# A two-layer hybrid trunk: opening the first FFN chunk by chunk, and other tiles in front of the mixers' late steps

## The chip, the cores and the metric

The kernel runs on one core of a Trainium2 chip. The metric is the device time of one execution in microseconds (us), lower is better. The time of the kernel before is the median of three runs.

## The reference, cut to what matters

The trunk has two layers for one sequence of S = 256 tokens with D = 1024 channels. Layer 0 is an FFN, a pooling and SSD mixer ("AB"), an FFN; layer 1 is an FFN, a multi-head latent attention ("MLA"), an FFN. Every sub-layer has its own shift, scale and gate, three rows of a matrix product with the vector `c`:

```python
c_act = jax.nn.silu(c)
for i in range(DEPTH):
    mod = c_act @ mod_w[i] + mod_b[i]
    sh1, sc1, g1, sh2, sc2, g2, sh3, sc3, g3 = jnp.split(mod, 3 * N_SUB, axis=-1)
    h = modulate(rmsnorm(x, norm_g[i, 0]), sh1, sc1)      # h * (1 + scale) + shift
    x = x + FFN_RES * g1[:, None, :] * swiglu(h, ffn_w13[i, 0], ffn_w2[i, 0])
    h = modulate(rmsnorm(x, norm_g[i, 1]), sh2, sc2)
    m = pool_ssd_mixer(h, ...) if i % 2 == 0 else mla_mixer(h, ...)
    x = x + g2[:, None, :] * m
    h = modulate(rmsnorm(x, norm_g[i, 2]), sh3, sc3)
    x = x + FFN_RES * g3[:, None, :] * swiglu(h, ffn_w13[i, 1], ffn_w2[i, 1])
return rmsnorm(x, final_norm_g)
```

`swiglu` is silu(h @ w1) * (h @ w3) @ w2 with 2816 inner channels. The SSD mixer ends in a norm over two groups of 512 channels and one output projection over 512 pooled and 1024 SSD channels. The attention has 16 heads, a causal mask and a softmax.

## The kernel before, in words

**Layout.** Activations lie transposed: 8 chunks of 128 channels on the partitions, 256 tokens along the free axis. Weights stream from HBM in tiles `raw` of 1 MiB (16 blocks of 128 x 128), six buffers, issued by SP in the order of a list `items`. Each half of a weight tile is split for exactness: ScalarE casts it to `wh` (L222), VectorE subtracts to get the rest, `wl` (L223), with five buffers of each; VectorE's subtraction waits for ScalarE's cast. The activation is split alike into `hh` and `hl`. One 128 x 128 product of a tile takes three matmuls (wl x hh, wh x hl, wh x hh, L522), or two where `hh` and `hl` lie side by side in `hx`: one of 512 columns (L266) and one of 256 (L267).

**Modulation.** A row of `mod_w` for one chunk of 128 channels is one VectorE instruction over 128 x 1024 with `c` (L210), which sums into one column of `modc`. These rows are items of the list too, set between the weights. `process_half` takes the next half item of the list, whatever it is; `take` hands out blocks and works ahead by four halves (one in the opening). A tile framework orders the instructions by their program order, pools and dependences; on TensorE, VectorE and ScalarE they run in that order.

**The opening** (`first_pairs`). The first FFN's first 16 output tiles of 256 columns (`n`, eight PSUM banks) are opened while `c`'s rows still come in. Chunks 0 and 1 of `h` are scaled (`scaled`, L500: scale L503, multiply L506, shift L293, then ScalarE's `h` L508 and cast L509) and meet f32 weight blocks directly (L532); then the other half of the tiles follows for these chunks (`part(1, 0)`); then three times a pair of chunks: four modulation rows, two `scaled`, two low parts (L512), four halves of weights, and `part` for all 16 tiles. Then the FFN goes on with full tiles `a` and `b` of 512 columns (L266, L267), and the down projection `f`, whose tiles end in VectorE's `residual` (L446).

**The AB mixer** runs a loop of eight turns: a transpose of `xs` (`tok_tile`), two heads' decay matrices, a `z` tile (in the turns 2 to 5), the products `y` (L818). After the first turn come the pooling tiles: `u`, its copy `utok`, then `pd` (L769) and `pw`. At turn 6 the first group norm is summed and its root taken by a Newton step on VectorE (`newton_r`). At the end some output tiles `o` are opened over their four pooled chunks (OPEN_A = 4 of 8, in three cuts CUT_A), while the second group's sum (`ss_g`, L321) and the split of its channels (`hx`, L315) are made; then all cuts are closed, each tile by two residual steps (L446) and the first steps of the next norm (`ul`, L376).

**The MLA mixer** makes q, k and v tiles, then eight turns of two heads: `scores` (`s`, L1077, softmax with Exp on ScalarE L1086, L1087), `attend_t` (transposes `pt`, copied to `pT` by ScalarE, L1099), a q tile for a later turn (`q_tiles`, with the copy `qr` L1058 and its rotation `rotq` L1005 on even turns), k tiles in the turns 0 and 1, `attend_o` (`o`, L1105, L1108). The output projection opens three tiles over six chunks after the loop, then finishes the last turn, then closes.

Of the kernel before, what the change touches and what calls it, by code (L numbers as in the profile page):

```python
# [61 lines left out]
def trunk(ctx, tc, xT, c_row, pos, kc, cols, rows, mod_w, w13s, w13, w2, win_a, wdt,  # L62
# [124 lines left out]
    def last_vector():  # L187
# [3 lines left out]
        return None  # L191

    def process_half():
# [10 lines left out]
        if it[0] == "m":  # L204
            _, l, v, b, halves = it
            hf = halves[hf]
            c0 = l * 72 + v * 8 + b * 2 + hf
# [6 lines left out]
            last = hf == halves[-1]  # L214
            done_mod[(l, v, 2 * b + hf)] = True
        else:
            lo, hi = hf * PT, min((hf + 1) * PT, it[2])
            n = (hi - lo) * P
            wh = wp.tile([P, PT * P], F32R, tag="wh", name=f"wh{i}_{hf}")
            wl = wp.tile([P, PT * P], F32R, tag="wl", name=f"wl{i}_{hf}")  # L220
            src = r[:, lo * P : hi * P]
            A.copy(wh[:, :n], src)  # L222
            V.tensor_tensor(out=wl[:, :n], in0=src, in1=wh[:, :n].bitcast(F32), op=ALU.subtract)  # L223
            pieces.append((wh, wl, hi - lo))
# [1115 lines left out]
```

## Time and profile before

| | us |
|---|---|
| three runs | 1026.05, 1029.26, 1035.23 |
| median | 1029.26 |
| the profiled execution's own time | 1032.29 |
| its span in the trace | 1030.5 |
| TensorE busy | 1010.1 (98%) |
| VectorE busy | 887.4 (86%) |
| ScalarE busy | 617.6 (60%) |

The span runs from the first to the last recorded instruction; 1.8 us lie around it. Times in the rows below count from the span's start. PE is TensorE, DVE VectorE, ACT ScalarE. The mean granted clock of TensorE is 0.993 of its full 2.4 GHz.

### The profile page before, as it was taken

The numbers are of one execution on the slowest core, as the hardware profiler recorded it, in microseconds if no ns is written. First come the engines' busy times: TensorE is split into PE (matmuls) and PEld (weight loads), VectorE is DVE, ScalarE is ACT, GpSimd is POOL, SyncE is SP. The second block draws the span as 40 slices with busy tenths as digits, with TensorE's granted clock in tenths as the row PEclk, the third lists the DMA queues.
The fourth block names the chain that finished last, engine by engine and source line by source line (L and its number), as shares of the span: only waits on it lengthen the run. The fifth ranks groups of instructions, "written<-read, shape, count | busy, mean of one in ns | idle before, by whom it ended". The sixth has DMA issues, their size and how long they took to land.

```text
span 1030.5 us, 16634 instructions
## 1 busy us (share of the span) xinstructions
PE 1010.1 (98%) x6300; PEld 895.1 (87%) x6300; DVE 887.4 (86%) x1665; ACT 617.6 (60%) x1124; POOL 0.2 (0%) x4
## 2 busy tenths in 40 slices
PE   9899999999999999999999999999999999999997
PEld 7898888889887988888898888889988798888886
DVE  6888999998998898989979988999988689877653
ACT  3475564448896666565447665555678666655542
POOL 0000000000000000000000000000000000000000
PEclk9999999999999999999999999999999999999999
DMA  9987989976743468788875887798643246766501
GB/s 353 397 311 283 354 296 377 342 294 223 261 164 123 164 227 304 273 296 332 300 262 176 316 292 264 298 342 304 247 175 118 77 164 220 270 214 236 184 21 41
DMA packets 38642, 254.93 MB, mean 247 GB/s; under 512 B 4241, under 2 KB 6817, under 8 KB 8738
## 3 DMA queue, kind: packets, MB, share of 16 engines
q1 hardware_dynamic: 38562, 253.88, 67.9%
q8 instruction: 49, 0.80, 0.3%
q14 instruction: 31, 0.25, 0.1%
HBM read 252.79 MB, written 1.06 MB: 246 GB/s over the span
## 4 chain that ended last, share of the span: by engine, by line
PE 85%; DVE 9%; ACT 3%; DMA 1%; issue 1%; SPq 0%; DVEq 0%; ACTq 0%
PE f L266 14%; PE a L266 13%; PE b L266 13%; PE f L267 7%; PE a L267 6%; PE b L267 6%; PE o L266 4%; DVE wl L223 3%; DVE raw L210 3%; PE o L267 2%; PE n L522 1%; PE s L1077 1%; DMA raw<-in_w13s 1%; PE u_a L260 1%; PE u_b L261 1%; PE u_a L261 1%
## 5 line engine op out<-in xcount | busy, mean ns | idle before, releaser
L222 ACT CAST wh<-raw 128x1024 fp32r<-128x1024 f32 x327 | 339.1, 1049 | 247.0 <-PE f L266 71.6
L223 DVE TENSOR_TENSOR wl<-raw,wh 128x1024 fp32r<-128x1024 f32 x327 | 396.2, 1218 | 77.8 <-ACT wh L222 77.3
L266 PE MATMUL f<-g,wh 128*128 128x512 f32 x704 | 245.7, 395 | 0.0
L266 PE MATMUL a<-hx,wh 128*128 128x512 f32 x568 | 202.9, 396 | 0.0
L266 PE MATMUL b<-hx,wh 128*128 128x512 f32 x568 | 202.7, 396 | 0.0
L267 PE MATMUL f<-g,wl 128*128 128x256 f32 x704 | 195.7, 279 | 1.1 <-DVE wl L223 1.1
L210 DVE SCALAR_TENSOR_TENSOR raw<-raw,c_bc 128x1024 f32<-128x1024 f32 x144 | 170.7, 1217 | 0.5 <-DMA raw<-in_mod_w 0.5
L266 PEld LDWEIGHTS f<-g,wh 128*128 128x128 f32 x704 | 131.9, 188 | 31.0
L267 PE MATMUL a<-hx,wl 128*128 128x256 f32 x568 | 158.4, 279 | 0.0
L267 PE MATMUL b<-hx,wl 128*128 128x256 f32 x568 | 158.4, 279 | 0.0
L267 PEld LDWEIGHTS f<-g,wl 128*128 128x128 f32 x704 | 132.4, 188 | 2.0 <-DVE wl L223 1.8
L266 PEld LDWEIGHTS b<-hx,wh 128*128 128x128 f32 x568 | 106.6, 188 | 25.3
L266 PEld LDWEIGHTS a<-hx,wh 128*128 128x128 f32 x568 | 106.6, 188 | 25.3 <-DVE hx L401 0.3
L267 PEld LDWEIGHTS a<-hx,wl 128*128 128x128 f32 x568 | 107.0, 188 | 0.3
L267 PEld LDWEIGHTS b<-hx,wl 128*128 128x128 f32 x568 | 107.0, 188 | 0.3
L266 PE MATMUL o<-hx,wh 128*128 128x512 f32 x128 | 47.2, 410 | 0.7 <-DVE hx L315 0.7
L375 ACT ACTIVATE uh<-xt,gs_t 128x256 fp32r<-128x256 f32 x40 | 20.3, 507 | 43.5 <-DVE xt L446 43.4
L314 ACT CAST g<-g 128x256 fp32r<-128x256 f32 x88 | 35.2, 404 | 17.2 <-DVE g L593 10.4
L522 PE MATMUL n<-hx,wh 128*128 128x256 f32 x224 | 41.9, 289 | 0.0
L446 DVE SCALAR_TENSOR_TENSOR xt<-f,gt_t,xt 128x256 f32<-128x256 f32 x64 | 30.7, 480 | 12.7 <-PE f L267 12.4
L315 DVE TENSOR_TENSOR g<-g,g 128x256 fp32r<-128x256 f32 x88 | 36.6, 418 | 1.9 <-ACT g L314 1.9
L522 PE MATMUL n<-hx,wl 128*128 128x256 f32 x112 | 32.9, 294 | 4.8 <-DVE wl L223 4.8
(397 smaller groups left out, 1683.5 us busy)
## 6 DMA issues: line engine op xcount, KB each, us to landing
raw<-in_w SPq DMA_DIRECT2D x124, 1024.0 KB, 5.0
raw<-in_mod_w SPq DMA_DIRECT2D x70, 1024.0 KB, 5.1
raw<-in_win_a SPq DMA_DIRECT2D x12, 1024.0 KB, 7.0
raw<-in_w13s SPq DMA_DIRECT2D x7, 1024.0 KB, 10.2
raw<-in_wout_a SPq DMA_DIRECT2D x6, 1024.0 KB, 4.7
raw<-in_wq SPq DMA_DIRECT2D x5, 1024.0 KB, 5.2
raw<-in_win_m SPq DMA_DIRECT2D x4, 1024.0 KB, 5.2
raw<-in_wo SPq DMA_DIRECT2D x4, 1024.0 KB, 4.8
```

The lines of the kernel that those rows point to most:

```text
L210: V.scalar_tensor_tensor(out=sl, in0=sl, scalar=1.0, in1=c_bc, op0=ALU.mult, op1=ALU.mult, accum_out=modc[:, c0 : c0 + 1])
L222: A.copy(wh[:, :n], src)
L223: V.tensor_tensor(out=wl[:, :n], in0=src, in1=wh[:, :n].bitcast(F32), op=ALU.subtract)
L260: T.matmul(pt, wl, xh, start=first, stop=False)
L261: T.matmul(pt, wh, xl, start=False, stop=False)
L266: T.matmul(pt, wh, x, start=first, stop=False)
L267: T.matmul(pt[:, S:], wl, x[:, 0], start=False, stop=last)
L314: A.copy(dh, src)
L315: V.tensor_tensor(out=dl, in0=src, in1=dh.bitcast(F32), op=ALU.subtract)
L375: A.activation(uh[:, c, :S], x, AF.Identity, bias=0.0, scale=g)
L446: V.scalar_tensor_tensor(out=xt[:, d], in0=pt[:, e * S : (e + 1) * S], scalar=gate[:, d : d + 1], in1=xt[:, d], op0=ALU.mult, op1=ALU.add)
L522: T.matmul(tile_of(m), w, x[:, k], start=k == 0 and m % 2 == 0 and w is wl, stop=k == NC - 1 and w is wh and x is hh, skip_group_check=True)
```

## The change

Opening: the items of the list are now, for each chunk, the scale row and the shift row together (two transfers of 0.5 MiB into one buffer) and one weight tile with all 16 output tiles' blocks of that chunk. A small table `colh` with what the opening needs is loaded first; the large one, `colt`, moves behind the opening's loads. The scale and the shift of a chunk are made by ScalarE. In each round `cast_half(1)` casts the weight halves ahead of their turn, and VectorE runs: two rows, the multiply, the first `wl`, the low part of `h`, the second `wl`. The low part of chunk 0 comes before the rows of chunk 1.

AB mixer: the first group norm moves from turn 6 to turn 5, behind the `z` tile; the pooling tiles from turn 1 to turn 2; six output tiles are opened for four. MLA mixer: the third k slab is made before the first scores, the fourth in turn 1; an Exp of one column stands before the scores; the output projection has three cuts (4, 6, 8), and its first tiles are opened in the turns 6 and 7, its last open tile before the last transposes. Two casts for the mask move in VectorE's order to their place in the program. The host lays out the weights for the new orders.

```diff
-CUT_A, OPEN_A = (4, 8, 12), 4
+CUT_A, OPEN_A = (4, 8, 12), 6
...
-G0_AT = 6
+G0_AT = 5
...
-CUT_M, OPEN_M = (6, 8), 3
+CUT_M, OPEN_M = (4, 6, 8), 3
...
     items = []
     for c in range(2):
-        items += [mod_block(0, 1, 0, (c,)), mod_block(0, 0, 0, (c,)),
-                  ("f", w13s[0, 0][:, 8 * P * c : 8 * P * c + 8 * P], 8)]
-    items.append(("w", w13s[1, 0], 16))
-    for b in range(1, 4):
-        items += [mod_block(0, 1, b), mod_block(0, 0, b)]
-        items += [("w", w13s[q, b], 16) for q in range(NSETS)]
+        items += [("m", ((0, 1, c), (0, 0, c))), ("f", w13s[0][:, 8 * P * c : 8 * P * c + 8 * P], 8)]
+    items.append(("w", w13s[1], 16))
+    for c in range(2, NC):
+        items += [("m", ((0, 1, c), (0, 0, c))), ("w", w13c[c - 2], 16)]
...
-    nc.sync.dma_start(colt, cols)
+    nc.sync.dma_start(colh, colsh)
     def late_loads():
+        nc.sync.dma_start(colt, cols)
...
+                (l, v, c), other = it[1]
+                if other == (l, v, c + 1):
+                    nc.sync.dma_start(r, mod_w[l, v, c // 2])
+                else:
+                    for e, (l, v, c) in enumerate(it[1]):
+                        nc.sync.dma_start(r[:, e * D : e * D + D], mod_w[l, v, c // 2][:, c % 2 * D : c % 2 * D + D])
...
+    def cast_half(ahead):
+        i = state["item"] + ahead
+        hf = state["cast"] if ahead else state["half"]
+        issue_dma(min([i] + held) + RAHEAD - 1)
+        it, r = items[i], raws[i]
+        lo, hi = hf * PT, min((hf + 1) * PT, it[2])
+        n = (hi - lo) * P
+        wh = wp.tile([P, PT * P], F32R, tag="wh", name=f"wh{i}_{hf}")
+        wl = wp.tile([P, PT * P], F32R, tag="wl", name=f"wl{i}_{hf}")
+        src = r[:, lo * P : hi * P]
+        A.copy(wh[:, :n], src)
+        state["cast"] = 1 - hf
+        return wh, wl, src, n
+
+    def low_half(c):
+        wh, wl, src, n = c
+        V.tensor_tensor(out=wl[:, :n], in0=src, in1=wh[:, :n].bitcast(F32), op=ALU.subtract)
+        pieces.append((wh, wl, n // P))
...
+        def scale(c):
+            A.activation(gs_t[:, 0, c : c + 1], modc[:, 8 + c : 9 + c], AF.Identity, bias=b1[:, c : c + 1],
+                         scale=colh[:, 16 + c : 17 + c])
...
+        scale(0)
...
         def scaled(c):
-            m, b = mod_col(0, 1, (c, c + 1))
-            g = gs_t[:, 0, c : c + 1]
-            V.scalar_tensor_tensor(out=g, in0=m, scalar=b1[:, c : c + 1], in1=colt[:, CP_NG + c : CP_NG + c + 1],
-                                   op0=ALU.add, op1=ALU.mult)
+            assert done_mod.get((0, 0, c)) and done_mod.get((0, 1, c))
+            g, sh = gs_t[:, 0, c : c + 1], sh_t[:, 0, c : c + 1]
             t = tmp(f"h{norm.key}_{c}")
             V.tensor_tensor(out=t, in0=xt[:, c], in1=r, op=ALU.mult)
-            sh = prep_shift(0, 0, (c, c + 1))[:, c : c + 1]
+            A.activation(sh, modc[:, c : c + 1], AF.Identity, bias=colh[:, c : c + 1])
             A.activation(h[c], t, AF.Identity, bias=sh, scale=g)
             A.copy(hh[:, c], h[c])
...
-        def part(q, b):
-            for m in range(8 * q, 8 * q + 8):
-                for k in (2 * b, 2 * b + 1):
-                    wh, wl = take()
-                    for w, x in ((wl, hh), (wh, hl), (wh, hh)):
-                        T.matmul(tile_of(m), w, x[:, k], start=k == 0 and m % 2 == 0 and w is wl,
-                                 stop=k == NC - 1 and w is wh and x is hh, skip_group_check=True)
+        def mm(m, k, w):
+            for w_, x in ((w[1], hh), (w[0], hl), (w[0], hh)):
+                T.matmul(tile_of(m), w_, x[:, k], start=k == 0 and m % 2 == 0 and w_ is w[1],
+                         stop=k == NC - 1 and w_ is w[0] and x is hh, skip_group_check=True)
 
         for c in range(2):
             if c:
                 process_half()
+                scale(1)
                 process_half()
             scaled(c)
             w = next_raw()
@@ -532,23 +554,25 @@
                 T.matmul(tile_of(m), w[:, m * P : (m + 1) * P], h[c], start=c == 0 and m % 2 == 0, stop=False,
                          skip_group_check=True)
             release_raw()
-        low(0)
+            if c == 0:
+                low(0)
         low(1)
-        process_half()
-        process_half()
-        part(1, 0)
-        for b in range(1, 4):
+        for m in range(8, 16):
+            for k in range(2):
+                mm(m, k, take())
+        for c in range(2, NC):
+            first = cast_half(1)
             process_half()
+            scale(c)
+            second = cast_half(1)
             process_half()
-            process_half()
-            scaled(2 * b)
-            process_half()
-            low(2 * b)
-            scaled(2 * b + 1)
-            process_half()
-            low(2 * b + 1)
-            for q in range(NSETS):
-                part(q, b)
+            scaled(c)
+            low_half(first)
+            low(c)
+            low_half(second)
+            skip_item()
+            for m in range(2 * NS):
+                mm(m, c, take())
...
-            if i == G0_AT:
-                r0 = newton_r("g0", gss[0], 1.0 / 512)
             if i < 8:
                 tok_tile(i)
                 nxt_h = (i, heads(i))
@@ -866,11 +888,13 @@
                 u_part(3)
             elif i < 6:
                 z_tile(i + 2)
+            if i == G0_AT:
+                r0 = newton_r("g0", gss[0], 1.0 / 512)
             ymm(*prev)
             if i < 5:
                 gate_y(i - 1)
             prev = nxt_h
-            if i == 1:
+            if i == 2:
...
+        d = sp.tile([P, 1], F32, tag="wsq", name="wexp", bufs=1)
+        A.activation(d, nqs[:, 0:1], AF.Exp)
...
+        k_tiles(2)
+        proj = OutProj(CUT_M, OPEN_M, lambda k: hx[:, k])
         prev = None
         for i in range(8):
             prs = scores(i)
@@ -1118,20 +1150,23 @@
                 attend_t(*prev)
             if i + NQ - 1 < 8:
                 q_tiles(i + NQ - 1)
-            if i < 2:
-                k_tiles(2 + i)
+            if i == 1:
+                k_tiles(3)
+            if i >= 6:
+                proj.part(i - 6, 0, CUT_M[0])
             if prev is not None:
                 attend_o(prev[0])
             prev = (i, prs)
         gate = prep_gate(l, 1)
         nxt = make_next()
 
-        proj = OutProj(CUT_M, OPEN_M, lambda k: hx[:, k])
         proj.target(gate, nxt)
-        proj.cut(0)
+        for d in range(2, OPEN_M):
+            proj.part(d, 0, CUT_M[0])
         attend_t(*prev)
+        proj.cut(1)
         attend_o(prev[0])
-        proj.cut(1)
+        proj.cut(2)
```

The order of the instructions on VectorE in the opening, from the third chunk on. Before (`raw` L210 rows of the modulation, `gs_t` scale, `h` the multiply, `sh_t` shift, `hx` low part, `wl` low weights):

```order
L210 SCALAR_TENSOR_TENSOR raw_197,modc<-raw_197,c_bc 128x1024 x2
L210 SCALAR_TENSOR_TENSOR raw_207,modc<-raw_207,c_bc 128x1024
L503 SCALAR_TENSOR_TENSOR gs_t<-modc,b_136,colt 128x1
L506 TENSOR_TENSOR h_0_2_297<-xt,r_first 128x256
L293 TENSOR_TENSOR sh_t<-modc,colt 128x1
L210 SCALAR_TENSOR_TENSOR raw_207,modc<-raw_207,c_bc 128x1024
L512 TENSOR_TENSOR hx<-h_190,hx 128x256
L503 SCALAR_TENSOR_TENSOR gs_t<-modc,b_136,colt 128x1
L506 TENSOR_TENSOR h_0_3_305<-xt,r_first 128x256
L293 TENSOR_TENSOR sh_t<-modc,colt 128x1
L223 TENSOR_TENSOR wl_0_313<-raw_210,wh_0_312 128x1024
```

And now, two rounds of one chunk each (L236 modulation, L530 multiply, L213 low weights, L536 low part):

```order
L236 SCALAR_TENSOR_TENSOR raw_172,modc<-raw_172,c_bc 128x1024 x2
L530 TENSOR_TENSOR h_0_2_302<-xt,r_first 128x256
L213 TENSOR_TENSOR wl_0_294<-raw_199,wh_0_293 128x1024
L536 TENSOR_TENSOR hx<-h_193,hx 128x256
L213 TENSOR_TENSOR wl_1_299<-raw_199,wh_1_298 128x1024
L236 SCALAR_TENSOR_TENSOR raw_210,modc<-raw_210,c_bc 128x1024 x2
L530 TENSOR_TENSOR h_0_3_372<-xt,r_first 128x256
L213 TENSOR_TENSOR wl_0_364<-raw_221,wh_0_363 128x1024
L536 TENSOR_TENSOR hx<-h_193,hx 128x256
```

The scale and shift rows are gone from VectorE, the first low weights stand behind two modulation rows instead of four, and the next rows only behind the second low weights.

The order on TensorE where the pooling tiles begin. Before, behind the last `u` product and one turn's `y`:

```order
L757 MATMUL u_2805<-wh_1_2898,hx 128x512
L818 MATMUL y_3014<-lm_2194,xtk_2189 64x256 x2
L821 MATMUL y_3014<-lm_2194,xtk_2190 64x128 x2
L769 MATMUL pd_3022<-raw_2644,utok 128x128
L770 MATMUL pd_3022<-raw_2644,utok 128x128
L771 MATMUL pd_3022<-raw_2644,utok 128x16
```

And now, one turn later, behind a `z` tile:

```order
L282 MATMUL z_3043<-hx,wh_0_2940 128x256
L842 MATMUL y_3073<-lm_2201,xtk_2195 64x256 x2
L845 MATMUL y_3073<-lm_2201,xtk_2196 64x128 x2
L793 MATMUL pd_3083<-raw_2650,utok 128x128
L794 MATMUL pd_3083<-raw_2650,utok 128x128
L795 MATMUL pd_3083<-raw_2650,utok 128x16
```

Between the last `u` product and the first `pd` there are now a further transpose, a `z` tile and a further `y`.

The order on ScalarE at the first scores of the attention (`pe` is the Exp, `qr` the copy that `rotq` reads, `qh` copies of q). Before:

```order
L1086 ACT_TABLE_LOAD
L1086 ACTIVATE pe_7844,st_8225<-s_8215,st_8225,rqs 128x128
L1087 ACTIVATE pe_7844,st_8225<-s_8215,st_8225,rqs 128x256
L1086 ACTIVATE pe_7844,st_8234<-s_8216,st_8234,rqs 128x128
L1087 ACTIVATE pe_7844,st_8234<-s_8216,st_8234,rqs 128x256
L1058 COPY qr<-qr_8243 128x256
L1061 COPY qr<-qn_8263 64x256
```

And now, first where the table is loaded, then the first scores:

```order
L1077 ACT_TABLE_LOAD
L1077 ACTIVATE wexp<-rqs 128x1
L1091 COPY qh<-qn_8162 64x256
L1092 COPY qh<-qn_8162 64x256
L207 CAST wh_0_8284<-raw_7949 128x1024
L1091 COPY qh<-qn_8196 64x256
```

```order
L1116 ACTIVATE pe_7850,st_8253<-s_8243,st_8253,rqs 128x128
L1117 ACTIVATE pe_7850,st_8253<-s_8243,st_8253,rqs 128x256
L1116 ACTIVATE pe_7850,st_8262<-s_8244,st_8262,rqs 128x128
L1117 ACTIVATE pe_7850,st_8262<-s_8244,st_8262,rqs 128x256
L207 CAST wh_1_8314<-raw_7949 128x1024
L1088 COPY qr<-qr_8271 128x256
```

The table load stands ahead of the first `qh` copies, and a weight cast stands between the Exp and the copy `qr`.

## Rows read from the trace of the kernel before

**Rows 1.** The page: busy us, share of the span, instructions of each engine.

```profile
PE 1010.1 (98%) x6300; PEld 895.1 (87%) x6300; DVE 887.4 (86%) x1665; ACT 617.6 (60%) x1124; POOL 0.2 (0%) x4
```

**Rows 2.** Waits of TensorE: tile, line, releaser; us in total, times, longest.

```profile
PE n L522 <- DVE wl L223: 4.8, 2, 3.6
PE u_B L261 <- DVE ul L376: 1.6, 1, 1.6
...
PE s L1077 <- DVE qh L1068: 0.9, 1, 0.9
PE ss_g L321 <- DVE gss L835: 0.9, 1, 0.9
PE rotq L1005 <- ACT qr L1058: 0.7, 1, 0.7
PE o L266 <- DVE hx L315: 0.7, 1, 0.7
...
PE pd L769 <- DVE utok L760: 0.6, 1, 0.6
PE o L1105 <- ACT pT L1099: 0.6, 2, 0.3
```

**Rows 3.** Windows: stretch, length; busy of each engine; PEclk, DMA share, GB/s.

```profile
22.05:27.75 5.70, 5.70 (x48) 5.67 (x47) 5.70 (x13) 1.01 (x2) 0.00 (x0) 1.00 1.01 415
32.57:35.99 3.42, 3.42 (x18) 3.42 (x18) 3.42 (x4) 0.68 (x1) 0.00 (x0) 0.50 1.01 422
...
150.00:218.00 68.00, 66.45 (x390) 57.71 (x388) 66.19 (x111) 30.57 (x45) 0.00 (x0) 1.00 0.94 348
220.31:223.72 3.41, 3.41 (x16) 3.24 (x15) 3.22 (x6) 2.20 (x3) 0.00 (x0) 0.50 0.92 348
315.88:319.29 3.41, 3.41 (x13) 2.92 (x12) 3.41 (x7) 0.56 (x2) 0.00 (x0) 0.50 0.25 41
```

**Rows 4.** Timelines of the opening: start us, length us, engine, line [idle before].

```profile
15.24 7.17 PE L532 MATMUL n<-h,raw 128*128 128x256 f32 x32
...
15.22 0.41 ACT L509 CAST hx<-h 128x256 fp32r<-128x256 f32 x1
...
17.41 0.60 ACT L508 ACTIVATE h<-h,sh_t,gs_t 128x256 f32<-128x256 f32 x1 [1.79 <-DVE sh_t L293]
...
29.36 3.89 ACT L222 CAST wh<-raw 128x1024 fp32r<-128x1024 f32 x4
...
30.43 1.23 DVE L223 TENSOR_TENSOR wl<-raw,wh 128x1024 fp32r<-128x1024 f32 x1 [2.05 <-ACT wh L222]
...
31.71 0.38 PE L522 MATMUL n<-hx,wl 128*128 128x256 f32 x1 [3.55 <-DVE wl L223]
...
58.04 3.49 DVE L223 TENSOR_TENSOR wl<-raw,wh 128x1024 fp32r<-128x1024 f32 x3
...
69.46 0.40 PE L266 MATMUL a<-hx,wh 128*128 128x512 f32 x1
```

**Rows 5.** VectorE's groups by line, 36 to 55 us: busy us, mean ns.

```profile
L210 DVE SCALAR_TENSOR_TENSOR raw<-raw,c_bc 128x1024 f32<-128x1024 f32 x8 | 9.5, 1219 | 0.0
...
L506 DVE TENSOR_TENSOR h<-xt,r_first 128x256 f32<-128x256 f32 x4 | 1.7, 419 | 0.0
```

**Rows 6.** VectorE's groups by line, 314 to 346 us.

```profile
L446 DVE SCALAR_TENSOR_TENSOR xt<-o,gt_t,xt 128x256 f32<-128x256 f32 x15 | 6.7, 477 | 0.1
```

**Rows 7.** Timelines of the attention: ScalarE's table load, TensorE's `o`.

```profile
761.19 1.28 ACT L1086 ACT_TABLE_LOAD   x1 [3.14 <-DVE st L1084]
...
800.12 0.65 PE L1105 MATMUL o<-pT,vt 128*64 128x256 f32 x4
...
803.85 0.81 PE L1105 MATMUL o<-pT,vt 128*64 128x256 f32 x3 [0.29 <-ACT pT L1099]
...
804.50 0.38 PE L1105 MATMUL o<-pT,vt 128*64 128x256 f32 x1
```

**Rows 8.** The page: loads by source, count, size, us from issue to landing.

```profile
raw<-in_w SPq DMA_DIRECT2D x124, 1024.0 KB, 5.0
```

More of the change, by code (lines that the diff above doesn't have):

```diff
@@ L61, in trunk @@
 @with_exitstack
-def trunk(ctx, tc, xT, c_row, pos, kc, cols, rows, mod_w, w13s, w13, w2, win_a, wdt,
+def trunk(ctx, tc, xT, c_row, colsh, pos, kc, cols, rows, mod_w, w13s, w13c, w13, w2, win_a, wdt,
           pool_w, wout_a, win_m, wkr, wkv, wq, wo, out):
@@ L90, in tmp, with mod_block @@
         return tp.tile([P, S], F32, tag="t", name=name)
-    def mod_block(l, v, b, halves=(0, 1)):
-        return ("m", l, v, b, halves)
+    def mod_block(l, v, b):
+        return ("m", ((l, v, 2 * b), (l, v, 2 * b + 1)))
     items = []
     for c in range(2):
-        items += [mod_block(0, 1, 0, (c,)), mod_block(0, 0, 0, (c,)),
-                  ("f", w13s[0, 0][:, 8 * P * c : 8 * P * c + 8 * P], 8)]
-    items.append(("w", w13s[1, 0], 16))
-    for b in range(1, 4):
-        items += [mod_block(0, 1, b), mod_block(0, 0, b)]
-        items += [("w", w13s[q, b], 16) for q in range(NSETS)]
+        items += [("m", ((0, 1, c), (0, 0, c))), ("f", w13s[0][:, 8 * P * c : 8 * P * c + 8 * P], 8)]
+    items.append(("w", w13s[1], 16))
+    for c in range(2, NC):
+        items += [("m", ((0, 1, c), (0, 0, c))), ("w", w13c[c - 2], 16)]
     mods = [(0, v) for v in (2, 4, 3, 5, 7, 6, 8)] + [(1, v) for v in (1, 0, 2, 4, 3, 5, 7, 6, 8)]
@@ L143, in trunk @@
     xt = cp.tile([P, NC, S], F32, name="xt")
+    colh = cp.tile([P, 24], F32, name="colh")
     modc = cp.tile([P, 144], F32, name="modc")
@@ L167, in trunk @@
     raws = {}
-    state = {"dma": 0, "item": 0, "half": 0, "pin": False}
+    state = {"dma": 0, "item": 0, "half": 0, "pin": False, "cast": 0}
     pieces, parked, held = [], [], []
@@ L191, in last_vector, with skip_item @@
         return None
+    def cast_half(ahead):
[15 more added lines that the diff above has]
+        pieces.append((wh, wl, n // P))
+    def skip_item():
+        raws.pop(state["item"])
+        state["item"] += 1
     def process_half():
@@ L204, in process_half @@
         if it[0] == "m":
-            _, l, v, b, halves = it
-            hf = halves[hf]
-            c0 = l * 72 + v * 8 + b * 2 + hf
+            l, v, c = it[1][hf]
+            c0 = l * 72 + v * 8 + c
             sl = r[:, hf * D : (hf + 1) * D]
@@ L213, in process_half @@
                 tc.add_manual_dep(last_vector(), prior.name, ORDER, reason="program order")
-            last = hf == halves[-1]
-            done_mod[(l, v, 2 * b + hf)] = True
+            last = hf == 1
+            done_mod[(l, v, c)] = True
         else:
             lo, hi = hf * PT, min((hf + 1) * PT, it[2])
[L218 to L224, printed above, removed]
+            low_half(cast_half(0))
             last = hi == it[2]
@@ L480, in first_pairs @@
         b1 = sp.tile([P, 8], F32, tag="b1", name="b1", bufs=1)
-        V.tensor_scalar(out=b1, in0=colt[:, CP_MODB + 8 : CP_MODB + 16], scalar1=1.0, scalar2=None, op0=ALU.add)
+        V.scalar_tensor_tensor(out=b1, in0=colh[:, 8:16], scalar=1.0, in1=colh[:, 16:24],
+                               op0=ALU.add, op1=ALU.mult)
+        def scale(c):
+            A.activation(gs_t[:, 0, c : c + 1], modc[:, 8 + c : 9 + c], AF.Identity, bias=b1[:, c : c + 1],
+                         scale=colh[:, 16 + c : 17 + c])
         pss = ps("ss_first")
@@ L938, in mixer_mla @@
         identb = sp.tile([P, P], BF16, tag="identb", name="identb", bufs=1)
+        prior = last_vector()
         V.tensor_copy(maskb, kct[:, KC_MSK : KC_MSK + P])
+        tc.add_manual_dep(last_vector(), prior.name, ORDER, reason="program order")
+        prior = last_vector()
         V.tensor_copy(identb, ident)
+        tc.add_manual_dep(last_vector(), prior.name, ORDER, reason="program order")
         for i in range(NQ):
@@ L1274, in _layout @@
     o["c_row"] = f["c"]
+    o["colsh"] = np.concatenate([_colv(f["mod_b"][0, :2 * D]), _colv(f["norm_g"][0, 0])], axis=1)
     o["pos"] = f["positions"]
@@ L1289, in _layout @@
     w = f["ffn_w13"].reshape(4, NC, P, 2, NJ, P).transpose(0, 4, 2, 3, 1, 5).reshape(4 * NJ, P, 16 * P)
-    s = w[:NS].reshape(NSETS, 4, P, 2, 4, 2, P).transpose(0, 4, 2, 1, 3, 5, 6).reshape(NSETS, 4, P, 8, 2, P)
-    s = np.ascontiguousarray(s)
-    s[0, 0] = s[0, 0].transpose(0, 2, 1, 3).reshape(P, 8, 2, P)
-    o["w13s"] = s.reshape(NSETS, 4, P, 16 * P)
+    s = w[:NS].reshape(NS, P, 2, NC, P).transpose(1, 3, 0, 2, 4).reshape(P, NC, 2 * NS, P)
+    o["w13s"] = np.stack([s[:, :2, :8].reshape(P, 16 * P),
+                          s[:, :2, 8:].transpose(0, 2, 1, 3).reshape(P, 16 * P)])
+    o["w13c"] = s[:, 2:].transpose(1, 0, 2, 3).reshape(NC - 2, P, 16 * P)
     o["w13"] = w[NS:]
```

4 lines of the change are left out of this document (1 added, 3 removed).

## The prediction

> **What bounds the kernel now.** I read the page first. TensorE is busy 98% of the span [rows 1]. So an edit pays only where TensorE stands still or runs slowly, and the most that all waits together can give is small. The second view is therefore the list of TensorE's waits [rows 2]: two waits of the opening's `n` tiles for low weight parts (4.8 us, the longer one 3.6), one of 1.6 for `ul` at the door of the SSD mixer, which the change doesn't touch, and then single waits of 0.3 to 0.9 us, three in the SSD mixer (`pd`, `ss_g`, `o` for `hx`) and four in the attention mixer (`s`, `rotq`, two `o` for `pT`). Third come the windows [rows 3]. The opening's parts run cleanly between 22.05 and 27.75 us: 48 matmuls of one group in 5.70 us. Right after the long wait, from 32.57, the granted clock is 0.50 (1.2 GHz of 2.4) for 3.42 us; after the 1.6 us wait it is 0.50 again from 220.31, and after the two waits in front of the SSD mixer's output from 315.88, each time for 3.41 us. Work done in a stretch at half clock takes twice its time, so each such stretch costs 3.42 / 2 = 1.7 us. Fourth, the opening's timeline [rows 4] says why the long wait arises: four ScalarE casts stand in a row behind the scaling of chunk 3 (29.36, 3.89 us for four), VectorE waits 2.05 us for the first of them, and only then makes `wl` at 30.43, for which TensorE has waited since 28.2.
>
> **The opening, before.** Its two f32 chunks begin at 15.24 and the first part at 22.05; the first full `a` tile starts at 69.46 [rows 3, 4]. Seven parts of 5.70 us would be 39.9 us and end at 61.95. The 7.5 us on top are 4.8 of waits, 1.7 of half clock, and 1.0 that I can't name row by row (short waits after the long ones).
>
> **The opening, after.** From chunk 2 on every chunk is one round: two modulation rows, one multiply for `h`, one low part of `h`, two `wl`. On VectorE that is 2 x 1.22 [rows 5] + 2 x 0.42 [rows 5] + 3.49 / 3 x 2 [rows 4] = 2.44 + 0.84 + 2.33 = 5.6 us by busy time; modulation rows overlap a little, so 5.6 is an upper bound. The scale and shift operations, four small ones per pair of chunks, leave VectorE for ScalarE, which has two casts (0.97 each), one `h` (0.60) and one cast of `h` (0.41) to do in a round [rows 4]: 3 us with the small ones, covered. TensorE needs 5.70 per round. So TensorE sets the pace by a tenth of a microsecond, and the casts no longer stand behind four things in a row, as the second half of the round is cast before its `h` is scaled. What is paid: the low part of `h` of chunk 0 now stands ahead of chunk 1's modulation rows on VectorE. It waits for ScalarE's cast, 15.22 + 0.41 = 15.6 [rows 4]; behind it come 0.42, two modulation rows 2.3, the multiply 0.4, ScalarE's `h` 0.60: 19.3. Chunk 0's 16 passes (half of the 32 that run from 15.24 [rows 4] to 22.05: 3.4 us) end at 18.5, as they start 0.2 earlier without the two small operations on VectorE. The big column table moves behind the opening's loads on SP's queue; that only brings the first weights nearer. TensorE thus waits 0.8 us where it did not, and the parts begin at 22.65. 22.65 + 39.9 = 62.55 against 69.46: **-6.9 us**. Bounds: if the unnamed 1.0 stays and one more half-clock stretch follows the new 0.8 us gap, -4.2; if the early low part costs nothing, -7.5. I take -6.9, as the clean window is the same six steps in the same pools. Behind the opening the first FFN keeps TensorE at 66.45 of 68.00 us with VectorE at 66.19 in 150 to 218 [rows 3]: VectorE is close to full there, but its work begins earlier by the same amount as the opening ends earlier, so I let the shift through.
>
> On the new gap the skill has a rule against me. By the rows the waits of 3.6 and 1.6 us and the close pair before 315.88 were followed by a drop of the clock [rows 2, 3]; the other single waits of up to 0.9 us [rows 2] stand in no stretch of half clock. The Trainium skill, "TensorE: Matmul & The Clock Gate", section "What's actually happening", says that the chip judges activity in windows which run freely against the program; by it where a gap falls decides, and one that did not cost the clock before may do so after a shift. By the rows the term is nothing, by the rule 1.7 us at worst; the lower bound above holds it.
>
> **The SSD mixer.** Three edits. Two more output tiles are opened (six for four) ahead of the group norm's end: their eight products (two tiles, 4 k-chunks) are 16 matmuls, at 66.45 / 390 = 0.17 us [rows 3] 2.7 us of TensorE work that needs only pool results and stands where `ss_g` waits 0.9 and `o` waits 0.7 for `hx` [rows 2]. Both fit in it, and the half-clock stretch from 315.88 follows from them [rows 3]: 0.9 + 0.7 + 1.7 = 3.3. The pool tiles move from the first to the second turn of the loop, so that a `z` tile lies between `utok`'s copy and `pd`, which waits 0.6 [rows 2]. The first group norm's sum moves to the fifth turn behind the `z` tile; its small chain on VectorE stands a turn earlier, with nothing late behind it. The two small mask casts that VectorE gets back in the attention mixer cost at most a multiply's 0.42 each [rows 5], beside TensorE's q tiles: nothing. Together **-3.9 us**. The price: six tiles then close one after the other, 1.4 us apart, and for each VectorE owes two residual steps (0.48 each [rows 6]), one `ul` of the same form and a sum of squares (0.4, as the multiplies of [rows 5]), 1.8 us, besides the `wl` for the last tiles. A backlog of up to 6 x 0.4 + 2 us builds, which the two tiles left (`d` = 6, 7) absorb before the next FFN needs `uh`, `ul`: nothing. If that cover is gone, up to 3.3 come back.
>
> **The attention mixer.** `s` waited 0.9 for `qh` [rows 2]; two `kn` tiles of the third k slab now stand in front of it, 12 matmuls of 256 columns, at 5.70 / 48 = 0.12 us [rows 3] 1.4 us: -0.9. `rotq` waited 0.7 for ScalarE's copy of `qr`, which was behind a table load of 1.28 us at 761.19 [rows 2, 7]. A one-column Exp loads that table before the scores. But a weight cast (0.97) now stands ahead of the copy; I leave 0.2 of the wait: -0.5. In the last two turns no `q` tiles are left, and `o` waits 0.29 for `pT` at 803.85 and its four long products stretch from 0.65 us (at 800.12) to 1.03 (0.81 + the fourth 0.38 apart) [rows 7]; the same again in the next turn [rows 2], which counts two waits. Opened output tiles (4 k-chunks, 8 matmuls, 1.4 us) now stand there: 2 x (0.29 + 0.38) = -1.3. Bounds of the three: 0 to -4. Sum **-2.7 us**.
>
> **Sum.** -6.9 - 3.9 - 2.7 = -13.5. The profiled execution took 1032.3 (its span 1030.5): 1018.8. It lies 3.0 above the median of the runs, 1029.26, and the same difference from there gives 1015.8. I take the middle, **1017.0**. A measurement of this kernel can tell 1%, 10.3 us: the line between faster and the same is at 1019.0, close to my forecast.
>
> **Rivals.** *B: VectorE is the opening's bound after all.* 5.6 against 5.70 us is thin; every wait for a cast or a load adds to it, and the first FFN, where VectorE is at 97%, could give the shift back. Then half of the 6.9 is lost: -10.0 at most, or if all is given back -6.6; with the middle, -8.3, 5.2 above my forecast: 1022.2. For it: the thin margin; against it: before, the same work fitted with scale and shift still on VectorE, and the waits were for order, not for sum. 14%.
>
> *C: the mixers' waits only move.* The opened tiles use the cover up early, and the close of six tiles waits for VectorE; in the attention mixer `pT` stays late. Then the opening alone counts, -6.9: 6.6 above my forecast, 1023.6. Against it: 2.7 us of cover for 1.6 of waits. 10%.
>
> *D, slower: the opening runs at the pace of single loads.* A chunk needs three transfers (two of 0.5 MiB for the modulation halves, one of 1 MiB), where before a pair of chunks had four of 1 MiB. A lone 1 MiB load takes 5.0 us from issue to landing [rows 8]; if the loads did not overlap, the 2 MiB of a chunk would take 10.0 us for 5.70 of work, 6 x 4.3 = 26 us more, 1043. It decides as soon as a chunk's 2 MiB take over 5.70 us, that is under 368 GB/s. Against it: 415 GB/s with the queues full at 1.01 of their share [rows 3], which is 5.05 us per chunk, and six buffers in flight. The Trainium skill, "DMA: Bandwidth & Descriptors", section "Anatomy of one DMA — SWDGE (gpsimd) path", gives 2.0 us fixed per transfer beside 436 GB/s for loads issued by GpSimd: one at a time a chunk would be an estimated 10.8 us. That agrees with the time of a lone load and not with the rate in the window, where several run together. 4%.
>
> **How the numbers follow.** My forecast 72%, its own range 1011 to 1022; nine tenths of it are beyond 1%. B 14%, C 10%, both within 1%; D 4%. Faster 0.64, the same 0.32, slower 0.04. The range, 1010 to 1026, holds the forecast, B and C.
>
> **What would show it.** First `a` tile near 62.5 us, TensorE without a wait over 1 us between 22 and 62 and no clock of 0.50 there; no clock of 0.50 near 310; neither `ss_g`, `pd`, `s` nor `o` for `hx` in the list of waits. Wrong if VectorE's `wl` still ends TensorE's waits in each chunk (B), if waits for residuals' tiles appear before the second FFN (C), or if casts wait for `raw` loads in the opening (D).

## The result, and the profile after

The changed kernel takes 1020.07 us (median of 6 runs, 1018.55 to 1023.13) against 1030.76 of the kernel before (6 runs): ratio 0.9899, 95% interval 0.9869 to 0.9929. A second set against 11 runs of before (label r_after below) gave 1019.83 and 0.9925 (0.9901 to 0.9949). So it is faster by about 1%, 8 to 11 us. Of all executions in this document one stands apart, 5614.41 us in one_block_out below; that kernel's ratio and median are without it.

The profiled execution has a span of 1018.4 us where before had 1030.5. TensorE's waits in it, by tile and releaser (us in total, times, longest), answer to [rows 2]:

```profile
PE f L287 <- DVE wl L213: 3.3, 3, 1.7
PE u_B L281 <- DVE ul L396: 1.6, 1, 1.6
PE warm L479 <- DVE eps_t L147: 1.0, 1, 1.0
PE rotq L1033 <- DVE wl L213: 0.9, 1, 0.9
PE y L842 <- DVE nw_g L368: 0.9, 1, 0.9
PE n L554 <- ACT h L532: 0.8, 2, 0.5
PE rotq L1033 <- ACT qr L1088: 0.4, 1, 0.4
PE u_B L280 <- ACT uh L395: 0.3, 1, 0.3
```

The 4.8 us of `n` for `wl` are gone, as are `s`, `ss_g`, `o` and `pd`. But `f` in the first FFN waits 3.3 us where it waited 1.1, and `rotq` 1.3 where it waited 0.7. The row of `f` in before:

```profile
PE f L267 <- DVE wl L223: 1.1, 2, 0.7
```

To see what that is worth I cut both spans at the same matmuls: the first `a` tile, the first `u_B`, the second FFN's first `a`, the end of the third FFN, the fourth FFN's first `a`, its end. Windows of before (length; busy time and count of each engine; clock, DMA):

```profile
69.46:211.77 142.31, 141.19 (x802) 122.21 (x801) 135.20 (x231) 73.07 (x123) 0.00 (x0) 1.00 0.89 324
211.77:362.72 150.95, 145.95 (x1029) 132.64 (x1029) 136.19 (x289) 111.23 (x222) 0.00 (x0) 0.98 0.55 197
713.59:852.29 138.70, 136.36 (x1006) 123.81 (x1006) 118.74 (x294) 98.42 (x223) 0.00 (x0) 1.00 0.44 156
852.29:1021.65 169.36, 169.36 (x961) 146.98 (x961) 119.47 (x189) 92.38 (x157) 0.00 (x0) 1.00 0.50 174
860.00:1000.00 140.00, 140.00 (x795) 121.36 (x794) 103.94 (x160) 81.20 (x138) 0.00 (x0) 1.00 0.58 201
```

The same of the changed kernel:

```profile
62.95:207.74 144.79, 141.46 (x802) 122.31 (x801) 136.61 (x237) 75.71 (x133) 0.00 (x0) 1.00 0.90 333
207.74:355.99 148.25, 145.33 (x1030) 131.44 (x1029) 135.35 (x289) 110.74 (x222) 0.00 (x0) 0.99 0.56 198
706.70:843.07 136.37, 135.09 (x1007) 123.37 (x1006) 119.70 (x297) 98.41 (x223) 0.00 (x0) 1.00 0.45 159
843.07:1009.42 166.35, 166.35 (x963) 146.70 (x962) 119.43 (x189) 92.53 (x157) 0.00 (x0) 1.00 0.51 177
860.00:1000.00 140.00, 140.00 (x810) 123.44 (x809) 101.97 (x155) 79.26 (x132) 0.00 (x0) 1.00 0.53 186
```

The start of the opening in the changed kernel (start, length, [idle before]; for before see [rows 4]):

```profile
14.87 0.48 PE L554 MATMUL n<-h,raw 128*128 128x256 f32 x1 [0.29 <-ACT h L532]
...
19.09 3.72 PE L554 MATMUL n<-h,raw 128*128 128x256 f32 x16 [0.50 <-ACT h L532]
22.46 0.47 PE L543 MATMUL n<-hx,wl 128*128 128x256 f32 x1
```

By stage: the opening -6.5 (69.46 to 62.95), the first FFN **+2.5**, the SSD mixer -2.7, the second and third FFN 0, the attention mixer -2.3, the fourth FFN -3.0; together -12.0. Three of these are not what they seem. The first `n` starts at 14.87 where before had 15.24, and that start varies from execution to execution (below): from the first `n` to the first `a` the opening takes 48.1 us in place of 54.2, -6.1. Before had two stretches of half clock in the SSD mixer (at 220.31 and 315.88 [rows 3]), the changed one a single one, at 215.75: 1.7 of the 2.7 is clock. And in the fourth FFN, where TensorE never waits and the clock is 1.00, the same matmuls simply ran faster: 810 in 140 us against 795.

### The profile page after: what moved, and what is told of

It is laid out like the page before. It is cut to its first block, busy times and chain, and to the rows that moved or that the text cites. A ratio compares the mean times of both kernels' runs of the same rounds, so it can differ in the third digit from the quotient of the medians.

```text
span 1018.4 us, 16658 instructions
## 1 busy us (share of the span) xinstructions
PE 1003.1 (99%) x6300; PEld 891.2 (88%) x6300; DVE 885.9 (87%) x1649; ACT 622.0 (61%) x1141; POOL 0.2 (0%) x4
## 4 chain that ended last, share of the span: by engine, by line
PE 92%; DVE 6%; ACT 1%; issue 0%; DVEq 0%; ACTq 0%
PE f L286 14%; PE a L286 13%; PE b L286 13%; PE f L287 7%; PE a L287 7%; PE b L287 7%; PE n L543 4%; PE o L286 4%; DVE raw L236 2%; DVE wl L213 2%; PE o L287 2%; PE s L1107 1%; PE u_a L281 1%; PE u_a L280 1%; PE u_b L281 1%; PE u_b L280 1%
## 5 line engine op out<-in xcount | busy, mean ns | idle before, releaser
L213 DVE TENSOR_TENSOR wl<-raw,wh 128x1024 fp32r<-128x1024 f32 x327 | 396.6, 1218 | 63.7 <-ACT wh L207 63.1
L236 DVE SCALAR_TENSOR_TENSOR raw<-raw,c_bc 128x1024 f32<-128x1024 f32 x144 | 170.7, 1216 | 0.2 <-DMA raw<-in_mod_w 0.2
L614 ACT COPY tb<-b 128x256 f32<-128x256 f32 x71 | 26.1, 368 | 18.2 <-PE b L287 18.0
```

The costliest lines, as they stand in the source:

```text
L236: V.scalar_tensor_tensor(out=sl, in0=sl, scalar=1.0, in1=c_bc, op0=ALU.mult, op1=ALU.mult, accum_out=modc[:, c0 : c0 + 1])
L614: A.copy(p, pt[:, S:])
```

## The experiments

The table has the same stage lengths for each kernel. A stage that an edit leaves alone repeats to 0.1 us in the first FFN and to 0.4 in the two mixers. The column "first a" counts from the span's start, and the first `n` starts anywhere from 14.0 to 15.2 us, with the old opening as with the new: differences below 1.2 us say little in that column. Beside the SSD mixer stands the number of half-clock stretches in it (1.7 us each), beside the attention the lengths of the later FFNs. "us" is the median; the ratio is to before in the same set and weighs all executions, so it is not that of the medians.

| kernel | first a | first FFN | SSD mixer | attention | FFN 2, 3, 4 | us | ratio (95%) |
|---|---|---|---|---|---|---|---|
| before | 69.46 | 142.3 | 150.95 (2) | 138.7 | 166.5, 166.5, 169.4 | 1027 to 1031 | 1 |
| changed | 62.95 | 144.8 | 148.25 (1) | 136.4 | 166.5, 166.5, 166.4 | 1020.07 | 0.9899 (0.9869 to 0.9929) |
| r_after | 63.11 | 144.8 | 148.31 (1) | 136.4 | 166.5, 166.5, 169.4 | 1019.83 | 0.9925 (0.9901 to 0.9949) |
| open_only | 63.32 | 144.8 | 147.71 (0) | 138.3 | 166.5, 169.5, 166.4 | 1025.52 | 0.9977 (0.9964 to 0.9989) |
| ab_only | 69.94 | 142.3 | 146.88 (0) | 138.4 | 166.5, 166.5, 166.3 | 1026.29 | 0.9992 (0.9979 to 1.0005) |
| mla_only | 69.43 | 142.3 | 150.95 (2) | 136.4 | 169.5, 169.5, 166.4 | 1026.15 | 0.9984 (0.9969 to 0.9999) |
| mods_moved | 63.31 | 140.5 | 150.54 (0) | 136.6 | 166.5, 166.5, 169.3 | 1021.84 | 0.9935 (0.9918 to 0.9953) |
| open_a4 | 62.51 | 144.7 | 148.04 (0) | 136.6 | 166.5, 166.5, 169.3 | 1022.11 | 0.9939 (0.9918 to 0.9959) |
| low_late | 62.55 | 144.8 | 146.78 (0) | 136.6 | 166.5, 166.5, 166.4 | 1019.10 | 0.9916 (0.9891 to 0.9941) |
| rot_late | 62.69 | 144.7 | 148.29 (1) | 135.0 | 166.5, 166.5, 166.4 | 1018.46 | 0.9900 (0.9879 to 0.9921) |
| both_late | 63.21 | 144.7 | 146.51 (0) | 135.2 | 166.5, 166.5, 166.3 | 1018.25 | 0.9898 (0.9878 to 0.9918) |
| one_block_in | 63.20 | 144.8 | 145.66 (0) | 134.9 | 166.5, 166.5, 166.4 | 1016.44 | 0.9901 (0.9871 to 0.9932) |
| one_block_out | 63.76 | 144.8 | 146.55 (0) | 134.9 | 166.5, 166.5, 169.4 | 1017.85 | 0.9896 (0.9875 to 0.9917) |
| old_turns | 63.41 | 144.7 | 146.21 (0) | 135.2 | 166.5, 166.5, 166.3 | 1017.19 | 0.9899 (0.9872 to 0.9925) |

**Each part alone.** Three kernels, each with one of the three parts of the diff.

> The new opening alone; both mixers as before. Theory: the first a tile comes near 63.0 us (69.5 before, 63.0 after), but the first FFN's down projection, in which VectorE is full, gives 2.5 of the 6.5 us back in waits of f for wl (3.3 us in all), so that the first u_B stands near 207.7 and the whole is 4.0 us shorter than before: ratio 0.996. Rival, the shift carries through and the 2.5 us were lost by other edits (the mask casts, the mixers' order): u_B near 205.2, 6.5 us shorter, 0.9937. Theory on the last FFN: its rate (795 matmuls in 140 us before, 810 after) is not set by the change's edits of the opening; it may come out at either value.

> The SSD mixer's three edits alone, the opening and the attention mixer as before. Theory: the half clock near 316 us and the waits of ss_g, o for hx and pd go, y for nw_g stays near 0.9: 2.7 to 3.9 us shorter than before, ratio 0.997. Rival: the wait only moves behind the mixer (u_a, u_b for ul): no change. Last FFN's rate: if it is a matter of the single execution, 795 or 810 matmuls in 140 us.

> The attention mixer's edits alone. Theory: s for qh and o for pT go, two waits of rotq stay near 1.3 us together: 2.6 us shorter, ratio 0.9975, with 795 matmuls in 140 us in the last FFN. Rival: the edits in front of the last FFN set its rate (810 in 140 us): 5.6 us shorter, ratio 0.9945.

The opening alone gives its whole gain at the first `a` tile (48.1 us from the first `n`, as in the changed kernel), and here too the first FFN gives 2.5 back: it is not the other edits. The SSD edits alone: the mixer without half-clock stretches is 146.88, against 147.71 in open_only, which has the old mixer and none either: -0.8. The attention edits alone: -2.0 to -2.3, with the fourth FFN's rate as in open_only and ab_only, which don't touch the attention: the rate does not follow from its edits. By the ratios the three are worth -2.4, -0.8 and -1.6 us, with intervals of 1.3 to 1.5 us on either side; expected were -4.0, -2.7 to -3.9 and -2.6, so each fell short. Together they are -4.8, less than the -7.7 of the whole change in r_after, but not beyond these intervals. The traces tell the parts apart far better.

**The changed kernel again.** The same file.

> The changed kernel once more, against more runs of before, with a second trace. Theory: the stage lengths repeat (first a tile near 63, u_B near 207.7, attention mixer 136.6 us from the last f tile of the third FFN to the first a tile of the fourth), while the rate of each later FFN (pairs of matmuls in 346.6 or 353.3 ns) and the half-clock stretches behind a wait are drawn anew in each execution. Without them the change is worth -6.3 + 2.5 - 1.1 - 2.0 = -6.9 us, with its share of half-clock stretches about -8: ratio 0.992. Rival, the last FFN's faster rate belongs to the change: ratio 0.990 or below, and 810 matmuls in 860 to 1000 us again.

All stage lengths repeat but the fourth FFN's, 169.4 in this execution and 166.4 in the first, of the same program. Windows of this trace:

```profile
560.00:640.00 80.00, 80.00 (x463) 69.94 (x463) 72.11 (x122) 48.00 (x87) 0.00 (x0) 1.00 0.81 291
860.00:1000.00 140.00, 140.00 (x795) 121.35 (x794) 100.85 (x154) 78.33 (x131) 0.00 (x0) 1.00 0.53 186
```

In open_only it is the third FFN that runs at the slower rate, and the fourth at the faster:

```profile
860.00:1000.00 140.00, 140.00 (x810) 123.44 (x809) 104.07 (x159) 81.19 (x138) 0.00 (x0) 1.00 0.56 196
560.00:640.00 80.00, 80.00 (x455) 69.43 (x454) 70.55 (x118) 47.00 (x85) 0.00 (x0) 1.00 0.80 287
```

So 3.0 of the 12.1 us between the two profiled executions belong to the execution, not to the change.

**Where the first FFN loses 2.5 us.**

```diff
-MODS = (10, 11, 3, 0, 8, 8, 8, 8, 3, 1, 4)
+MODS = (10, 8, 6, 0, 8, 8, 8, 8, 3, 1, 4)
```

> The changed kernel with three of the 11 modulation blocks of the first FFN's down projection moved into the SSD mixer's input projection (3 becomes 6): 6 x 1.15 = 6.9 us of VectorE leave the down projection. Theory, VectorE's fullness there gives the opening's gain back: the waits of f for wl (3.3 us) go below 1 and u_B stands 2 to 3 us earlier than in the changed kernel (207.7); the whole 1 to 3 us shorter than it, less what the mixer's VectorE then makes late. Rival, the waits come from the order of residual steps in front of the low weights and not from the sum: the waits stay above 2.5.

The waits of `f` vanish and the FFN shrinks by 4.3 us: 3.3 are these waits, and TensorE's own work takes 1.0 less (140.5 us for 141.5); the mixer, with 6.9 us more on VectorE, pays 3.9 of them (it would be 146.6 without). That looked like my theory, but a smaller step of the same kind did not: one_block_in (10, 10, 4) and one_block_out (10, 10, 3, 1), both on top of the late edits below, leave the first FFN at 144.8. Their mixers don't grow (145.66 and 146.55): in both the 1.6 us wait of `u_B` is gone, and in one_block_out `o` waits 2.2 for `hx` instead.

> Both late edits, and one modulation block (2 x 1.15 us of VectorE) moved from the first FFN's down projection to the SSD mixer's input projection. Theory: VectorE's sum sets the first FFN's end, so the stage from the first a to u_B shrinks by about 2 us (144.8 to 142.8) and the mixer grows by less than 1.5. Rival, the mixer pays it all back (three blocks shortened the FFN by 4.3 and lengthened the mixer by 3.9).

> Both late edits, and one modulation block moved from the first FFN's down projection to the SSD mixer's output projection. Theory: the first FFN shrinks by 2 us as with the block in the input projection, and the six opened tiles leave VectorE room for 2.3 us more: the mixer grows by less than 1. Rival: VectorE is as full there (residuals, low parts): the mixer grows by 2.

So VectorE's sum alone is not the cause. By the windows above TensorE is busy for 141.2 us of the first FFN before and for 141.5 now; the rest of the stage is the waits of `f`, 1.1 and 3.3. The changed kernel's VectorE timeline in the down projection (start, length, [idle before]):

```profile
169.70 1.00 DVE L466 SCALAR_TENSOR_TENSOR xt<-f,gt_t,xt 128x256 f32<-128x256 f32 x2
173.39 0.48 DVE L466 SCALAR_TENSOR_TENSOR xt<-f,gt_t,xt 128x256 f32<-128x256 f32 x1 [2.70 <-PE f L287]
173.80 0.47 DVE L396 SCALAR_TENSOR_TENSOR ul<-xt,gs_t,uh 128x256 fp32r<-128x256 f32 x1
174.19 0.41 DVE L403 TENSOR_TENSOR ss<-ss,sq 128x256 f32<-128x256 f32 x1
174.53 1.22 DVE L236 SCALAR_TENSOR_TENSOR raw<-raw,c_bc 128x1024 f32<-128x1024 f32 x1
...
176.81 2.35 DVE L213 TENSOR_TENSOR wl<-raw,wh 128x1024 fp32r<-128x1024 f32 x2
```

VectorE stands still for 2.70 us, waiting for TensorE to finish the fourth tile of `f`; behind that wait it still owes `ul`, two modulation rows and the next `wl`, and TensorE runs dry for 1.7 us. The two later waits of 0.8 each stood in before too, as 0.7 and 0.4. The program's order on VectorE shows why; before, around the residual steps (`xt<-f`) of the third and fourth tile (`f_1833` here is `f_1839` below):

```
L446 SCALAR_TENSOR_TENSOR xt<-f_1763,gt_t,xt 128x256 x2
L376 SCALAR_TENSOR_TENSOR ul<-xt,gs_t,uh 128x256
L383 TENSOR_TENSOR ss_1_1614<-ss_1_1614,sq_1_2_1830 128x256
L210 SCALAR_TENSOR_TENSOR raw_1696,modc<-raw_1696,c_bc 128x1024 x2
L223 TENSOR_TENSOR wl_0_1853<-raw_1738,wh_0_1852 128x1024
L223 TENSOR_TENSOR wl_1_1873<-raw_1738,wh_1_1872 128x1024
L446 SCALAR_TENSOR_TENSOR xt<-f_1833,gt_t,xt 128x256
```

and in the changed kernel:

```
L466 SCALAR_TENSOR_TENSOR xt<-f_1769,gt_t,xt 128x256 x2
L466 SCALAR_TENSOR_TENSOR xt<-f_1839,gt_t,xt 128x256
L396 SCALAR_TENSOR_TENSOR ul<-xt,gs_t,uh 128x256
L403 TENSOR_TENSOR ss_1_1620<-ss_1_1620,sq_1_2_1836 128x256
L236 SCALAR_TENSOR_TENSOR raw_1702,modc<-raw_1702,c_bc 128x1024 x2
L213 TENSOR_TENSOR wl_0_1859<-raw_1744,wh_0_1858 128x1024
L213 TENSOR_TENSOR wl_1_1879<-raw_1744,wh_1_1878 128x1024
```

Nothing in the FFN's code was edited. The framework's scheduler, starting from another opening, set the first residual step of the fourth tile ahead of six other instructions; open_only has this order, ab_only and mla_only, with the old opening, do not. VectorE's residual group in the stretch 140 to 215 us (idle before, last column) tells the kernels apart. In before, whose FFN is 142.3 long:

```profile
L446 DVE SCALAR_TENSOR_TENSOR xt<-f,gt_t,xt 128x256 f32<-128x256 f32 x14 | 6.7, 480 | 0.0
```

In one_block_in, 144.8:

```profile
L466 DVE SCALAR_TENSOR_TENSOR xt<-f,gt_t,xt 128x256 f32<-128x256 f32 x16 | 7.6, 476 | 2.7 <-PE f L287 2.7
```

and in mods_moved, 140.5:

```profile
L466 DVE SCALAR_TENSOR_TENSOR xt<-f,gt_t,xt 128x256 f32<-128x256 f32 x16 | 7.7, 481 | 0.1
```

That row goes with the length in all fourteen traces: the ten with 2.7 us of idle have 144.7 or 144.8, and before, ab_only and mla_only (142.3) and mods_moved have none. A kernel that moves this one step back alone was not tried; mods_moved moves it and the six rows together.

**Two tiles fewer.** `OPEN_A` 6 to 4 in the changed kernel.

> The changed kernel with four opened output tiles in the SSD mixer in place of six. Theory: the waits of ss_g (0.9) and of o for hx (0.7) come back near 310 us and the mixer from the first u_B to the second FFN's first a tile grows by 1 to 1.6 us, and by 1.7 more if the clock falls behind them in this execution; ratio to before 0.993 to 0.995. Rival: the later turns of the loop (group norm, pooling tiles) cover them, nothing comes back.

The mixer is 148.04 against 146.78 and 146.51 with six tiles (no half clock in any): the two tiles are worth 1.3 to 1.5. The wait that returns is one, `o` for `hx`; `ss_g` stays away:

```profile
PE o L286 <- DVE hx L335: 1.5, 1, 1.5
```

**The old turns.** Undone on top of both late edits: the group norm's sum and the pooling tiles go back to the turns 6 and 1, six tiles stay.

> Both late edits, six opened tiles, but the group norm's sum and the pooling tiles in the turns they had before (6 and 1). Theory: these two moves gained nothing (the mixer was 147.71 us with the old turns and four tiles, 148.04 with the new turns and four tiles, no half-clock stretch in either): the mixer comes to 146.3 to 146.8 from the first u_B to the second FFN's first a tile. Rival: with the old turns pd waits 0.6 again and the mixer is 0.5 us longer than the 146.7.

146.21 against 146.51, and with four tiles 147.71 (open_only) against 148.04: the two moves gained nothing; that they cost 0.3 is about the scatter of this stage. With the old turns `pd` waits again (0.6), but the 64 `y` products keep TensorE busy for 9.3 us, in the new turns for 10.5, and `y` waits 0.7 for the Newton step, in the new turns 0.9. In old_turns and then in both_late:

```profile
L841 PE MATMUL y<-lm,xtk 128*64 128x256 f32 x32 | 5.8, 404 | 0.7 <-DVE nw_g L364 0.7
L844 PE MATMUL y<-lm,xtk 128*64 128x128 f32 x32 | 3.5, 274 | 0.0
...
L841 PE MATMUL y<-lm,xtk 128*64 128x256 f32 x32 | 6.5, 404 | 0.9 <-DVE nw_g L368 0.9
L844 PE MATMUL y<-lm,xtk 128*64 128x128 f32 x32 | 4.0, 276 | 0.0
```

**The low part of chunk 0.** Put back behind chunk 1's f32 matmuls.

```diff
-            if c == 0:
-                low(0)
+        low(0)
         low(1)
```

> The changed kernel with the low part of chunk 0 put back behind chunk 1's f32 matmuls. Theory: the wait of n for h at 19 us (0.5, with its slower restart 0.8) goes and the first a tile comes 0.8 us earlier, near 62.2; but the first FFN ends where VectorE lets it, so that u_B stands less than 0.3 us earlier than the 207.7 of the changed kernel. Rival: the shift carries through, u_B near 206.9; or the parts then wait for the low part and nothing is won at the a tile.

From the first `n` to the first `a` this kernel takes 47.3 us; the six traces with the early low part take 48.1 to 48.3. So the 0.8 us are won here, as the theory had it. But the four later kernels, which have the same opening, take 48.0 to 49.4 (first `a` at 63.20 to 63.76): nothing is won reliably. In three of them the wait stands one step on, and all three start their first `n` early, at 14.0 to 14.4 us, where low_late starts at 15.23. In both_late:

```profile
PE n L543 <- ACT hx L533: 0.9, 1, 0.9
```

**The rotation.** The changed kernel's second `rotq` waits 0.9; the list names `wl`, but ScalarE's timeline shows the copy `qr` at 772.84, behind a weight cast and two Exps, and `rotq` starts at 773.29, 0.05 after its end:

```profile
770.90 1.08 ACT L207 CAST wh<-raw 128x1024 fp32r<-128x1024 f32 x1
771.85 0.49 ACT L1116 ACTIVATE pe<-s,st,rqs 128x128 f32<-128x128 f32 x1
...
772.30 0.59 ACT L1117 ACTIVATE pe<-s,st,rqs 128x256 f32<-128x256 f32 x1
...
772.84 0.40 ACT L1088 COPY qr<-qr 128x256 f32<-128x256 f32 x1
```

```diff
             if prev is not None:
                 attend_o(prev[0])
+            if i + NQ - 1 < 8:
+                q_rot(i + NQ - 1)
```

Here `q_rot` is the last part of `q_tiles`: the rotation and the sums behind it.

> The changed kernel with the rotation of q (rotq and the sums behind it) issued after the products o of the previous turn instead of before. Theory: rotq at 773 us waits 0.9 for ScalarE's copy qr, which stands behind a weight cast and the Exp; 0.8 us of o products in front of it take that: the attention mixer (136.6 us) gets 0.8 to 1.0 shorter, the wait at 758 (0.4) stays, as there is no o in the first turn. Rival: the wait moves to s for qh, or ScalarE is the bound there, and the length stays.

The attention mixer is 135.0 for 136.4: -1.4, more than expected. Only the wait of 0.4 in the first turn stays.

**Both late edits.**

> The changed kernel with both late edits (the low part of chunk 0 behind chunk 1's f32 matmuls; q's rotation behind the previous turn's o). Stage lengths as in the two single runs: first a near 62.5, first FFN 144.8, SSD mixer 146.7 without a half-clock stretch, attention mixer 135.0. Theory: 1.5 us shorter than the changed kernel; ratio to before 0.990. Rival: the two interact (the starts shift the loads), and less is left.

They add up as single lengths (135.2, 146.5); the time is 1018.25. The shortest of all is one_block_in with 1016.44 and a span of 1014.6: there `u_B` for `ul` no longer waits, and with it goes what the clock may take behind that wait. Two of its six executions took 1022 and 1025 us and its ratio has the widest interval of the four kernels with both late edits, so that it beats the changed kernel by stage lengths, not beyond the noise of the times.

## Why the prediction was right, and where its steps were not

Forecast 1017.0 with a range of 1010 to 1026; measured 1020.07 and 1019.83. The direction and the size hold; of the four terms two hold, and two errors and one piece of luck make up the rest. All signs that were set for the forecast came, and none for a rival; none of them looked at the first FFN, where 2.5 us were lost.

**The opening (-6.9): right, -6.5** at the first `a` tile (62.5 to 63.8 in the eleven traces with the new opening, 62.55 forecast), -6.1 from the first `n`. From there on TensorE has no wait over 0.9 us in it and no half clock. The 0.8 us that I charged to the early low part are there: from the first `n` to the first part it takes 7.6 us, before 6.8. The seven parts took 40.5 us where I had 39.9.

**"I let the shift through": the step that failed.** The first FFN gave 2.5 of the 6.5 back, in every kernel with the new opening but mods_moved, which has another order. The work did begin earlier by the shift, but not in the same order. Rival B named the place of the loss, with too large a size (half of 6.9, or all) and the wrong cause: VectorE wasn't full, it stood still for 2.70 us at a residual step that the scheduler had moved forward.

**The SSD mixer (-3.9): mis-sized.** 0.8 to 1.2 us without the clock: the two tiles -1.3 or more, as forecast for the waits (1.6), the turns nothing to +0.3 where I had -0.6: the wait of `pd` went, and the `y` products took 1.2 longer. The third part, 1.7 for the stretch at half clock, I had taken for certain. It came behind the pair `ss_g` and `o` in before and mla_only, but not in open_only, where the same pair waits 0.9 and 0.7:

```profile
PE ss_g L341 <- DVE gss L859: 0.9, 1, 0.9
PE o L286 <- DVE hx L335: 0.7, 1, 0.7
```

By these three traces, which are few, the chance is about two in three, worth 1.1, not 1.7. The backlog of residual steps that rival C feared did not show.

**The attention mixer (-2.7): right, -2.0 to -2.3.** `s` and `o` went as worked out. The 0.2 left for `rotq` behind a weight cast was mis-sized: 1.3 was there. With it the working gives -1.6, so the rest brought 0.4 to 0.7 more than worked out, and no row names that.

**Luck.** -6.1 + 2.5 - 0.9 - 2.1 is -6.6 with the opening's clock stretch in it; with 1.1 for the other it is -7.7, which is r_after's ratio (-7.7) and less than the first set's (-10.4). The forecast stood for -12.3 (1029.26 to 1017.0); the middle of its two sums, 1018.8 and 1015.8, is 1017.3. The sum from one profiled execution hit 1018.8 against the 1020.18 of the changed one's own only because the fourth FFN drew its slower rate before and its faster rate after. Rival D had no part: in the opening, no wait of TensorE names a load.

## What to carry to other kernels

Cut two traces at the same matmuls, the first one behind the start-up, and compare stage lengths: they repeat to a few tenths of a us where times of whole runs scatter by several, and they show at once that what an early stage wins can be lost in one that nobody edited. Where a scheduler orders an engine, look at its order in all later stages, above all for an instruction that waits for a whole tile and has come to stand in front of what that tile's successor needs. Count a half-clock stretch behind a wait by its chance and not as certain.
